# Weight splits further ahead in the MLP of a two-layer encoder trunk, paid for with one raw tile and one set of rotary tables

## The chip, the cores and the metric

The kernel runs on 1 core of a Trainium2 chip. The metric is the device time of one execution in microseconds (us). Before the change it is 2003.32 us, the median of 3 runs (2003.09 to 2005.98). The trace comes from one more execution, of 2003.99 us, whose profiled span is 2002.2 us.

## What is computed

256 tokens of width 2048 go through two layers in float32. Each layer normalises, makes one input projection whose columns belong to three attention groups (A: windowed, B: neighbourhood on a grid, C: global with normalised and rotated q and k), joins them through an output projection, and ends with a squared-ReLU MLP of hidden width 8192:

```python
for l in range(DEPTH):
    h = rmsnorm(x, norm_mix[l])
    proj = jnp.einsum('bsd,de->bse', h, w_in[l])
    ...
    x = x + jnp.einsum('bse,ed->bsd', mix, w_o[l])
    h = rmsnorm(x, norm_mlp[l])
    u = jax.nn.relu(jnp.einsum('bsd,df->bsf', h, w_up[l]))
    x = x + jnp.einsum('bsf,fd->bsd', u * u, w_down[l])
return rmsnorm(x, norm_final)
```

The rotary part of group C multiplies q and k with cosines and sines that are scaled by the gains `c_q_gain[l]` and `c_k_gain[l]`; the kernel keeps these products as tables.

## The kernel before

**Steps.** All four big products are a list of steps. A step loads 512 KB of weights into a raw tile (`load`, SP's DMA queue, tile `wraw`), splits it into a high and a low part (`split`: ScalarE casts `whi`, L1017; VectorE subtracts to get `wlo`, L1018), and multiplies both on TensorE (`mm`). The input projection's and output projection's steps are matmuls of L479, 12 of 128x512 each. The main loop at the end of the function issues, ahead of the matmuls of a step, the loads of up to six steps behind it (`LOOK_LOAD` = 7 counts the step itself) and the split of the next step (`LOOK_SPLIT` = 2). Where the running step has `fourth=False`, which are the steps of the MLP mix, the next two are split.

**Tiles.** There are five raw tiles, three `whi` and three `wlo`. Outside the MLP every fourth split goes into a further pair of tiles, `spare0` and `spare1`; in the MLP the same two tiles hold the weights B11 of the products.

**The MLP.** `up_steps` makes the hidden activations: a step has 8 matmuls of 512 columns (L679) and 8 of 256 (L684), and after every fourth step `evac` copies the result out (L657 on ScalarE, L658 on VectorE, then L659 to L666, L696 to L698 on both). `strassen_steps` makes half of the down projection by seven products P1 to P7 in place of eight (the Strassen-Winograd scheme), each in two halves h = 0, 1 (a and b below) of 6 matmuls (L801). Its weights are B11, sums of weight blocks (`sum_of`, L779, VectorE) and blocks that a DMA from GpSimd's queue adds onto a tile (`on_top`, L783). T1 is B11 + B12 and T2 is B22 + (B11 + B12) with blocks stored so that sums stand for differences; P2 reads its own block, P6 reads T2. A step's `look` says how many steps ahead its sum is made: 8 in general, 3 for the sum T1 (at P2), 5 − h for T2 (at P6). The steps are dealt out by a pattern: 22 steps, 14 of products and 8 of the up projection, make a half group, in the order P1a P2a U P1b P2b U P6a P6b U P7a U P7b P5a U P5b P4a U P4b P3a U P3b U. There are twelve half groups in a layer, then two groups with other patterns. When a product group is done, VectorE adds its bank onto x (`evac`, which calls `residual`, L221); the score banks `S` take turns.

**Order.** The order on each engine follows from the program's order and a scheduler that places instructions by their dependences. A few edges are written out: `sum_of` is issued after the last subtract, the table code after the last subtract at step 11. In each engine's queue the order is then fixed, and an instruction that waits holds up those behind it.

**Rotary tables.** `setup_tables` makes four pairs of tables once, `ctab` and `stab` for q and k of both layers (L133, L136), at about 41 us. `rope` reads them on GpSimd (L317 and L321).

Of the kernel before, what the change touches and what calls it, by code (L numbers as in the profile page):

```python
# [17 lines left out]
F32 = mybir.dt.float32  # L18
# [5 lines left out]
P = 128  # L24
D = 2048
L = 2
# [17 lines left out]
def tile_trunk(ctx: ExitStack, tc: tile.TileContext, x_in, xt_in, w_in, w_o, w_up, w_down,  # L44
# [29 lines left out]
    def spare(dt, h):  # L74

        return wp.tile([P, 2, 512], dt, tag=f"spare{h}", bufs=1, name=nm("spare"))
# [47 lines left out]
    def setup_tables():  # L124

        nc.vector.tensor_scalar(negsink, rp[:, :, 0:8], -1.0, None, op0=ALU.mult)
        for l in range(L):
            nc.vector.tensor_scalar(rp[:, l, 8:72], rp[:, l, 8:72], 0.125, None, op0=ALU.mult)
            for which, off in (("q", 8), ("k", 72)):
                g = rp[:, l:l + 1, off:off + 64]  # L130
                c = cp.tile([P, NT, 64], F32, name=f"ctab_{which}{l}")
                s = cp.tile([P, NT, 64], F32, name=f"stab_{which}{l}")
                nc.vector.tensor_mul(c, cos_t, g.to_broadcast([P, NT, 64]))  # L133
                for a in range(4):
                    b = a ^ 1
                    nc.vector.tensor_mul(s[:, :, 16 * a:16 * a + 16], sin_t[:, :, 16 * a:16 * a + 16],  # L136
                                         g[:, :, 16 * b:16 * b + 16].to_broadcast([P, NT, 16]))
                ctab[which, l], stab[which, l] = c, s
# [159 lines left out]
    def rope(raw, H, which, l, outs):  # L298
# [15 lines left out]
        ct, st = ctab[which, l], stab[which, l]  # L314
# [149 lines left out]
    class Step:  # L464


        def __init__(self, src, kk, n, pre, mm, fourth=True, loads=None, prep=None, raw=None,
                     look=0, ready=None):
            self.look, self.ready = look, ready
            self.src, self.kk, self.n, self.pre, self.mm, self.fourth = src, kk, n, pre, mm, fourth  # L470
            self.loads, self.prep, self.raw = loads or [], prep, raw
# [31 lines left out]
    def layer_steps(l):  # L503
# [143 lines left out]
        def up_steps(g):  # L647

            out_ = []
            for q in range(4 * g, 4 * g + 4):  # L650
# [18 lines left out]
                for s in range(4):  # L669
# [19 lines left out]
                    out_.append(Step(w_up[l, q * 4 + s], 4, 256, pre, mm, fourth=False))  # L689
# [10 lines left out]
        def down_steps(gs, j, ks=range(4)):  # L700
# [7 lines left out]
            for n, (g, k) in enumerate(tiles):  # L708
# [40 lines left out]
                out_.append(Step(w_down[l, ti], 2, 512, None, mm, fourth=gs == (7,)))  # L749
            return out_  # L750

        def strassen_steps(g, pair=0):
# [35 lines left out]
            for (name, lf, bk, fresh, dst), h in first + then:  # L788
                def mm(wh, wl, name=name, lf=lf, bk=bk, fresh=fresh, dst=dst, h=h):
# [14 lines left out]
                    if h == 1 and (name != "P2" or g == (5 if pair else 7)):  # L804
                        evac(o, *dst)
                        if g == 7 and name in ("P3", "P4"):
                            layer_end(l, dst[1])
                loads, prep, get, ready, look = [], None, None, None, 8
                if name == "P1":
                    loads = [(("B11", h), src(0, 0, h), lambda h=h: spare(F32, h))]  # L810
                    get = lambda h=h: raw["B11", h]
                elif name == "P2":
# [5 lines left out]
                    look = 3  # L818
# [6 lines left out]
                elif name == "P6":  # L825
# [6 lines left out]
                    look = 5 - h  # L832
# [14 lines left out]
                stp = Step(src(1, 0, h) if name == "P2" else None, 2, 512, None, mm, fourth=False, prep=prep,  # L847
# [143 lines left out]
    fourth = [0]  # L991

    def load(i, halves=False):
# [7 lines left out]
        w = wp.tile([P, s.kk, s.n], F32, tag="wraw", bufs=5, name=nm("wraw"))  # L1001
# [21 lines left out]
    warm = cp.tile([P, 512], F32R, name="warm")  # L1023
# [21 lines left out]
    for i in range(8):  # L1045
        load_xt()
        if i < 5:
            load(i, halves=i == 0)
    nl = 5
# [3 lines left out]
    for i, s in enumerate(steps):  # L1053
# [159 lines left out]
```

## Time and profile before

| quantity | value |
|---|---|
| median of 3 runs | 2003.32 us |
| profiled execution / its span | 2003.99 / 2002.2 us |
| TensorE matmul busy | 1976.5 us |
| VectorE busy | 1689.7 us |
| ScalarE busy | 1302.4 us |
| GpSimd busy | 381.2 us |
| mean DMA rate | 223 GB/s |

In the rows, PE is TensorE's matmul, PEld its weight load, DVE VectorE, ACT ScalarE, POOL GpSimd, and SPq a queue of DMA issues. A row of the timeline gives the start, the time taken, engine, line, operation, output<-inputs, and in brackets how long the engine was idle before it and on what it waited. A row of waits gives the total of a wait in us, how often it occurred and the longest. A row of windows gives the length of a stretch, the busy time of PE, PEld, DVE, ACT and POOL in it, the granted clock of TensorE (1.00 is full), the share of DMA time and GB/s. The page's DMA issues list the size and the median time from issue to landing.

### The profile page before, as it was taken

How to read it: one execution, taken by the hardware profiler on the slowest of the kernel's cores; microseconds unless marked ns; L12 is line 12 of the kernel's file. 1: busy time of each engine (PE TensorE's matmuls, PEld its weight loads, DVE VectorE, ACT ScalarE, POOL GpSimd, SP SyncE). 2: the span in 40 equal slices, each digit the busy share in tenths (PEclk: the TensorE clock that was granted, in tenths of full speed). 3: DMA queues.
4: the chain of work that ended last, by engine and by line, in shares of the span. 5: the costliest groups of instructions: out<-in, count | busy, mean ns of one | idle time of the engine just before them, and what ended most of it. 6: DMA issues, size and time to landing. Idle time of an engine off the chain costs nothing.

```text
span 2002.2 us, 28385 instructions
## 1 busy us (share of the span) xinstructions
PE 1976.5 (99%) x10054; PEld 1667.0 (83%) x10054; DVE 1689.7 (84%) x2119; ACT 1302.4 (65%) x1814; POOL 381.2 (19%) x444
## 2 busy tenths in 40 slices
PE   9999999999999999999999999999999999999998
PEld 7888888888888888888888888888888888888886
DVE  7777877899999999988857688778999999999887
ACT  7667756666666666666657677566666666666664
POOL 0674520000100001000008655100010000000000
PEclk9999999999999999999999999999999999999999
DMA  9755656788888878877756465557888888888774
GB/s 342 216 158 157 212 169 191 215 250 234 255 251 261 241 242 247 246 233 222 228 185 197 148 184 192 179 189 226 235 255 251 263 241 239 247 247 268 221 228 139
DMA packets 125753, 445.80 MB, mean 223 GB/s; under 512 B 14339, under 2 KB 16643, under 8 KB 125612
## 3 DMA queue, kind: packets, MB, share of 16 engines
q1 hardware_dynamic: 109052, 384.18, 56.7%
q0 software_dynamic: 16128, 58.73, 16.3%
q8 instruction: 79, 1.29, 0.3%
q10 hardware_dynamic: 432, 1.10, 0.1%
q14 instruction: 62, 0.51, 0.1%
HBM read 438.16 MB, written 2.11 MB: 220 GB/s over the span
## 4 chain that ended last, share of the span: by engine, by line
PE 92%; DVE 3%; ACT 3%; issue 1%; DMA 0%; SPq 0%; POOLq 0%; POOL 0%; DVEq 0%; ACTq 0%
PE mm L479 28%; PE mm L679 23%; PE S L801 21%; PE mm L684 12%; PE tr L801 4%; DVE wlo L1018 2%; ACT whi L1017 2%; PE tr L388 1%; PE tr L407 1%; PE S L351 1%; PE S L350 1%; PE tr L231 1%; ACT wide L657 0%; PE tr L263 0%; PE tr L400 0%
## 5 line engine op out<-in xcount | busy, mean ns | idle before, releaser
L1018 DVE TENSOR_TENSOR wlo<-wraw,whi 128x1024 fp32r<-128x1024 f32 (+1 forms) x481 | 592.0, 1233 | 146.0 <-ACT whi L1017 141.0
L1017 ACT CAST whi<-wraw 128x1024 fp32r<-128x1024 f32 (+1 forms) x481 | 502.9, 1048 | 240.1 <-PE mm L679 79.2
L679 PE MATMUL mm<-big,whi 128*128 128x512 f32 x2048 | 514.7, 391 | 0.0
L679 PEld LDWEIGHTS mm<-big,whi 128*128 128x128 f32 x2048 | 382.4, 188 | 79.8 <-ACT whi L1017 0.7
L479 PE MATMUL mm<-whi,big 128*128 128x512 f32 (+1 forms) x1404 | 423.4, 384 | 1.0 <-ACT whi L1017 1.0
L801 PE MATMUL S<-whi,big 128*128 128x512 f32 x1344 | 369.9, 397 | 9.7 <-ACT whi L1017 9.7
L479 PEld LDWEIGHTS mm<-whi,big 128*128 128x128 f32 x1404 | 260.2, 189 | 50.5 <-ACT whi L1017 2.3
L684 PEld LDWEIGHTS mm<-big,wlo 128*128 128x128 f32 x2048 | 279.7, 190 | 20.5
L684 PE MATMUL mm<-big,wlo 128*128 128x256 f32 x2048 | 286.2, 282 | 0.0
L801 PEld LDWEIGHTS S<-whi,big 128*128 128x128 f32 x1344 | 235.3, 189 | 59.8 <-ACT whi L1017 20.5
L479 PE MATMUL mm<-wlo,big 128*128 128x512 f32 (+1 forms) x702 | 253.8, 381 | 0.0
L783 POOL DMA_DIRECT2D side<-in_w_down_dram x56 | 48.9, 873 | 1001.9 <-ACT whi L1017 612.1
L801 PE MATMUL S<-wlo,big 128*128 128x512 f32 x672 | 210.9, 395 | 1.4
L1017 ACT CAST whi<-big 128x1024 fp32r<-128x1024 f32 x112 | 118.2, 1055 | 126.6 <-DVE big L779 58.4
L1018 DVE TENSOR_TENSOR wlo<-big,whi 128x1024 fp32r<-128x1024 f32 x112 | 136.7, 1221 | 44.0 <-ACT whi L1017 44.0
L1018 DVE TENSOR_TENSOR wlo<-side,whi 128x1024 fp32r<-128x1024 f32 x112 | 136.6, 1220 | 31.5 <-ACT whi L1017 31.2
L801 PEld LDWEIGHTS S<-wlo,big 128*128 128x128 f32 x672 | 124.9, 188 | 37.6 <-DVE wlo L1018 11.0
L1017 ACT CAST whi<-spare 128x1024 fp32r<-128x1024 f32 x112 | 117.7, 1051 | 53.0 <-PE S L801 41.7
L479 PEld LDWEIGHTS mm<-wlo,big 128*128 128x128 f32 x702 | 132.4, 189 | 23.4 <-DVE wlo L1018 0.3
L1017 ACT CAST whi<-side 128x1024 fp32r<-128x1024 f32 x112 | 117.5, 1049 | 46.5 <-PE S L801 42.9
L1018 DVE TENSOR_TENSOR wlo<-spare,whi 128x1024 fp32r<-128x1024 f32 x112 | 136.5, 1219 | 6.8 <-ACT whi L1017 6.6
L479 PE MATMUL mm<-spare,big 128*128 128x512 f32 (+1 forms) x606 | 140.3, 381 | 0.0
(153 smaller groups left out, 2224.2 us busy)
## 6 DMA issues: line engine op xcount, KB each, us to landing
wraw<-in_w_up_dram SPq DMA_DIRECT2D x256, 512.0 KB, 4.7
wraw<-in_w_in_dram SPq DMA_DIRECT2D x119, 512.0 KB, 3.8
side<-in_w_down_dram SPq DMA_DIRECT2D x112, 512.0 KB, 4.7
wraw<-in_w_down_dram SPq DMA_DIRECT2D x88, 512.0 KB, 5.3
wraw<-in_w_o_dram SPq DMA_DIRECT2D x64, 512.0 KB, 3.7
spare<-in_w_down_dram SPq DMA_DIRECT2D x56, 512.0 KB, 5.6
side<-in_w_down_dram POOLq DMA_DIRECT2D x56, 512.0 KB, 7.4
big<-in_w_down_dram POOLq DMA_DIRECT2D x56, 512.0 KB, 7.3
```

Source lines behind the costliest of these rows:

```text
L231: nc.tensor.transpose(psv[:, kk, t, :], x[:, t, c0:c0 + P], ident)
L350: nc.tensor.matmul(o, st, u.kh[:, kh, :], start=True, stop=False)
L351: nc.tensor.matmul(o, st, u.kl[:, kh, :], start=False, stop=True)
L388: nc.tensor.transpose(ps[:, c * P:(c + 1) * P], u.p[:, s, kb * P:(kb + 1) * P], ident)
L407: nc.tensor.matmul(ps, u.V[:, kb, u.kv, :, :], pt[:, kb, :], start=n == 0, stop=n == 3)
L479: nc.tensor.matmul(banks[t][:, 0:n], a, (wl if part == "hl" else wh)[:, i, :], start=first and i == 0 and part == "hh", stop=last and i == ...
L679: nc.tensor.matmul(box["b"][fs], wh[:, kk, fs * P:(fs + 1) * P], ht, start=s == 0 and kk == 0, stop=False, skip_group_check=True)
L684: nc.tensor.matmul(box["b"][fs][:, 0:256], wl[:, kk, fs * P:(fs + 1) * P], ht[:, 0:256], start=False, stop=s == 3 and kk == 3, skip_group_ ...
L783: nc.gpsimd.dma_start(tile, src(par, j, h).rearrange("p (k n) -> p k n", k=2), accum_op=ALU.add)
L801: nc.tensor.matmul(o, ops[i][a], w[:, i, :], skip_group_check=True, start=fresh and h == 0 and i == 0 and a == 0 and w is wh and (bk != "b ...
L1017: last_act[0] = nc.scalar.copy(h[:, part], w[:, part]).ins
L1018: last_lo[0] = nc.vector.tensor_sub(lo[:, part], w[:, part], f(h[:, part])).ins
```

## The change

Four `whi` and four `wlo` tiles take the place of three each; the trick with every fourth split goes, and `spare` becomes `first`, which holds B11 alone. `wraw` has four tiles, not five. A step marked `deep` (up projection, products, and the plain down steps that are not of the last group alone) has the next three steps split ahead of its matmuls; any other step has the next one. The sums for P2 and P6 get looks of 8 and 6. The rotary tables exist once for q and once for k; `layer_tables(1)` remakes them for the second layer at a place in the program late in layer 0's MLP. The tile `warm` moves to another pool, and the start loads four raw tiles ahead.

```diff
-    def spare(dt, h):
-        return wp.tile([P, 2, 512], dt, tag=f"spare{h}", bufs=1, name=nm("spare"))
+    def first_block(h):
+        return wp.tile([P, 2, 512], F32, tag=f"first{h}", bufs=1, name=nm("first"))
...
-        for l in range(L):
-            nc.vector.tensor_scalar(rp[:, l, 8:72], rp[:, l, 8:72], 0.125, None, op0=ALU.mult)
-            for which, off in (("q", 8), ("k", 72)):
...
-                ctab[which, l], stab[which, l] = c, s
+        nc.vector.tensor_scalar(rp[:, :, 8:72], rp[:, :, 8:72], 0.125, None, op0=ALU.mult)
+        for which in ("q", "k"):
+            ctab[which] = cp.tile([P, NT, 64], F32, name=f"ctab_{which}")
+            stab[which] = cp.tile([P, NT, 64], F32, name=f"stab_{which}")
+        layer_tables(0)
+
+    def layer_tables(l):
+        for which, off in (("q", 8), ("k", 72)):
+            g = rp[:, l:l + 1, off:off + 64]
+            c, s = ctab[which], stab[which]
+            nc.vector.tensor_mul(c, cos_t, g.to_broadcast([P, NT, 64]))
+            for a in range(4):
+                b = a ^ 1
+                nc.vector.tensor_mul(s[:, :, 16 * a:16 * a + 16], sin_t[:, :, 16 * a:16 * a + 16],
+                                     g[:, :, 16 * b:16 * b + 16].to_broadcast([P, NT, 16]))
...
                         evac(o, *dst)
+                        if (l, g, name) == (0, 7, "P1"):
+                            layer_tables(1)
...
-                    loads = [(("B11", h), src(0, 0, h), lambda h=h: spare(F32, h))]
+                    loads = [(("B11", h), src(0, 0, h), lambda h=h: first_block(h))]
...
-                    look = 3
                     ready = lambda h=h: ("P1", h) in done
...
-                    look = 5 - h
+                    look = 6
...
-        w = wp.tile([P, s.kk, s.n], F32, tag="wraw", bufs=5, name=nm("wraw"))
+        w = wp.tile([P, s.kk, s.n], F32, tag="wraw", bufs=4, name=nm("wraw"))
...
-        fourth[0] += s.fourth
-        if s.fourth and fourth[0] % 4 == 0:
-            h, lo = [spare(F32R, e).rearrange("p k n -> p (k n)").rearrange("p (k n) -> p k n", k=s.kk) for e in range(2)]
-        else:
-            h = wp.tile([P, s.kk, s.n], F32R, tag="whi", bufs=3, name=nm("whi"))
-            lo = wp.tile([P, s.kk, s.n], F32R, tag="wlo", bufs=3, name=nm("wlo"))
+        h = wp.tile([P, s.kk, s.n], F32R, tag="whi", bufs=4, name=nm("whi"))
+        lo = wp.tile([P, s.kk, s.n], F32R, tag="wlo", bufs=4, name=nm("wlo"))
...
-    warm = cp.tile([P, 512], F32R, name="warm")
+    warm = mid(F32R, 512)
...
-        if i < 5:
+        if i < 4:
             load(i, halves=i == 0)
-    nl = 5
+    nl = 4
...
-        while ns < min(len(steps), i + LOOK_SPLIT + (not s.fourth)):
+        while ns < min(len(steps), i + LOOK_SPLIT + 2 * s.deep):
```

Line numbers shift by four in the functions behind the tables: L779, L783, L801, L221 and L657 become L783, L787, L805, L225 and L661; the cast and the subtract stay at L1017 and L1018, the loads of L1004 become L1008 and those of the tiles L1001.

Three places of the order show what moves. The first is a half group of the MLP on VectorE, from the sums T1 (onto `spare` or `first`) and T2 (into `big`) to the subtracts of the halves of P6 (`wlo<-big`); `x<-S` is the evacuation. Before:

```order
L1018 TENSOR_TENSOR wlo_4591<-wraw_4528,whi_4590 128x1024 [waits DMAHW1_49,PE_49,Activation_49]
L779 TENSOR_TENSOR spare_4502<-spare_4502,side_4526 128x1024 [waits DMAHW5_49,DVE_49]
L779 TENSOR_TENSOR big_4595<-side_4564,spare_4439 128x1024 [waits DMAHW2_49]
L1018 TENSOR_TENSOR wlo_4615<-wraw_4541,whi_4614 128x1024 [waits DMAHW3_49,PE_49,Activation_49]
L221 SCALAR_TENSOR_TENSOR x<-S_3807,rsq,x 128x512 [waits PE_49]
L1018 TENSOR_TENSOR wlo_4628<-big_4595,whi_4627 128x1024 [waits Activation_49]
L779 TENSOR_TENSOR big_4631<-side_4576,spare_4502 128x1024 [waits DMAHW4_49]
L658 TENSOR_TENSOR wide_4661<-wide_4661,mm_4508 128x256 [waits Activation_49]
L1018 TENSOR_TENSOR wlo_4641<-big_4631,whi_4640 128x1024 [waits Activation_49]
```

and after:

```order
L1018 TENSOR_TENSOR wlo_4569<-wraw_4518,whi_4568 128x1024 [waits DMAHW2_49,PE_49,Activation_49]
L783 TENSOR_TENSOR first_4491<-first_4491,side_4516 128x1024 [waits DMAHW4_49,DVE_49]
L783 TENSOR_TENSOR big_4572<-side_4553,first_4428 128x1024 [waits DMAHW1_49]
L1018 TENSOR_TENSOR wlo_4583<-wraw_4531,whi_4582 128x1024 [waits DMAHW4_49,PE_49,Activation_49]
L783 TENSOR_TENSOR big_4586<-side_4566,first_4491 128x1024 [waits DMAHW3_49,DVE_49]
L1018 TENSOR_TENSOR wlo_4606<-big_4572,whi_4605 128x1024 [waits PE_49,Activation_49]
L225 SCALAR_TENSOR_TENSOR x<-S_3797,rsq,x 128x512 [waits PE_49]
L1018 TENSOR_TENSOR wlo_4619<-big_4586,whi_4618 128x1024 [waits Activation_49]
L1018 TENSOR_TENSOR wlo_4630<-wraw_4580,whi_4629 128x1024 [waits DMAHW5_49,PE_49,Activation_49]
L662 TENSOR_TENSOR wide_4650<-wide_4650,mm_4498 128x256 [waits Activation_49]
```

P6b's sum moved ahead of P6a's subtract, both subtracts of P6 and the next one moved ahead of the additions of the up-projection's copy (L658, now L662), and the evacuation moved behind P6a's subtract. ScalarE in the same place, with the casts of P6a, P6b and of the next up step, and the copies L657; before:

```order
L1017 CAST whi_4614<-wraw_4541 128x1024 [waits DMAHW3_49,DVE_49,PE_49]
L1017 CAST whi_4627<-big_4595 128x1024 [waits DVE_49,PE_49,Activation_49]
L657 COPY wide_4661<-mm_4508 128x256 [waits PE_49]
L657 COPY wide_4661<-mm_4509 128x256 [waits PE_49]
L1017 CAST whi_4640<-big_4631 128x1024 [waits DVE_49,Activation_49]
```

and after:

```order
L1017 CAST whi_4582<-wraw_4531 128x1024 [waits DVE_49,DMAHW4_49,PE_49,Activation_49]
L1017 CAST whi_4605<-big_4572 128x1024 [waits DVE_49,PE_49,Activation_49]
L1017 CAST whi_4618<-big_4586 128x1024 [waits DVE_49,PE_49,Activation_49]
L1017 CAST whi_4629<-wraw_4580 128x1024 [waits DMAHW5_49,PE_49,Activation_49]
L1017 CAST whi_4664<-side_4464 128x1024 [waits DMASW0_49,PE_49,Activation_49]
L661 COPY wide_4650<-mm_4498 128x256 [waits PE_49]
```

The two copies no longer stand between the two casts of P6, but behind four casts.

The second place is SP's queue at the start, which issues the tokens' tiles (`big<-in_xt_dram`), the weights and x. Before:

```order
L1034 DMA big_127<-in_xt_dram 128x512 [waits DMAHW2_49]
L1004 DMA wraw_129<-in_w_in_dram 128x1024 [waits DMAHW3_49]
L1034 DMA big_131<-in_xt_dram 128x512 [waits DMAHW4_49]
L1034 DMA big_133<-in_xt_dram 128x512 [waits DMAHW5_49]
L1034 DMA big_135<-in_xt_dram 128x512 [waits DMAHW6_49]
L1004 DMA wraw_157<-in_w_in_dram 128x1024 [waits DMAHW7_49,DVE_49]
```

and after:

```order
L1034 DMA big_127<-in_xt_dram 128x512 [waits DMAHW2_49]
L1034 DMA big_129<-in_xt_dram 128x512 [waits DMAHW3_49]
L1034 DMA big_131<-in_xt_dram 128x512 [waits DMAHW4_49]
L1034 DMA big_133<-in_xt_dram 128x512 [waits DMAHW5_49]
L1001 DMA first_3635<-in_w_down_dram 128x1024 [waits DMAHW6_49]
L1001 DMA first_3705<-in_w_down_dram 128x1024 [waits DMAHW7_49]
L1008 DMA wraw_155<-in_w_in_dram 128x1024 [waits DMAHW0_49,DVE_49]
L1008 DMA wraw_157<-in_w_in_dram 128x1024 [waits DMAHW1_49,DVE_49]
```

The fifth weight tile (`wraw_129`, now `wraw_155`) moved behind the last token tiles and behind the first two blocks B11 of the MLP (`first`), whose tiles nothing else uses.

The third place is VectorE in layer 0's mixing stage, where the remade tables stand, though the code calls for them in the MLP (L138 and L141 are the tables, with two pieces of what is around them):

```order
L1018 TENSOR_TENSOR wlo_876<-wraw_687,whi_875 128x1024 [waits DMAHW1_49,DVE_49,Activation_49]
L377 TENSOR_TENSOR sm_777<-sm_767,negsink 128x4 [waits DVE_49]
L138 TENSOR_TENSOR ctab_k<-cs,rp 128x128 [waits Pool_49]
L141 TENSOR_TENSOR stab_k<-cs,rp 128x2x16 [waits Pool_49] x4
L1018 TENSOR_TENSOR wlo_910<-wraw_705,whi_909 128x1024 [waits DMAHW2_49,Activation_49]
```

and further on, for q:

```order
L435 SCALAR_TENSOR_TENSOR big_1335<-mid_1171,gn,big_1335 128x256 [waits Activation_49] x2
L138 TENSOR_TENSOR ctab_q<-cs,rp 128x128 [waits Pool_49]
L141 TENSOR_TENSOR stab_q<-cs,rp 128x2x16 [waits Pool_49] x4
L361 TENSOR_REDUCE sm_1392<-S_1382 128x4 [waits PE_49]
L1018 TENSOR_TENSOR wlo_1452<-wraw_1289,whi_1451 128x1024 [waits DMAHW4_49,Activation_49]
```

Both table rows wait for GpSimd, and subtracts and softmax rows stand behind them; before the change VectorE has no tables here.

More of the change, by code (lines that the diff above doesn't have):

```diff
@@ L313, in rope @@
         t2 = big(F32, NT, H, 64)
-        ct, st = ctab[which, l], stab[which, l]
+        ct, st = ctab[which], stab[which]
         for t in range(NT):
@@ L464, in tile_trunk, with __init__ @@
     class Step:
-        def __init__(self, src, kk, n, pre, mm, fourth=True, loads=None, prep=None, raw=None,
+        def __init__(self, src, kk, n, pre, mm, deep=False, loads=None, prep=None, raw=None,
                      look=0, ready=None):
             self.look, self.ready = look, ready
-            self.src, self.kk, self.n, self.pre, self.mm, self.fourth = src, kk, n, pre, mm, fourth
+            self.src, self.kk, self.n, self.pre, self.mm, self.deep = src, kk, n, pre, mm, deep
             self.loads, self.prep, self.raw = loads or [], prep, raw
@@ L687, in mm @@
                             evac()
-                    out_.append(Step(w_up[l, q * 4 + s], 4, 256, pre, mm, fourth=False))
+                    out_.append(Step(w_up[l, q * 4 + s], 4, 256, pre, mm, deep=True))
             return out_
@@ L748, in down_steps @@
                 ti = (g * 4 + j) * 4 + k
-                out_.append(Step(w_down[l, ti], 2, 512, None, mm, fourth=gs == (7,)))
+                out_.append(Step(w_down[l, ti], 2, 512, None, mm, deep=gs != (7,)))
             return out_
```

11 lines of the change are left out of this document (1 added, 10 removed).

## The prediction

> **What bounds the kernel.** First the page's span, the busy times and the chain that ended last.
>
> ```profile
> span 2002.2 us, 28385 instructions
> PE 1976.5 (99%) x10054; PEld 1667.0 (83%) x10054; DVE 1689.7 (84%) x2119; ACT 1302.4 (65%) x1814; POOL 381.2 (19%) x444
> PE 92%; DVE 3%; ACT 3%; issue 1%; DMA 0%; SPq 0%; POOLq 0%; POOL 0%; DVEq 0%; ACTq 0%
> ```
>
> TensorE carries 92% of the chain. The change leaves its matmuls alone, so it can only win or lose time in which TensorE waits; VectorE's and ScalarE's 6% of the chain are such places. The view of waits names the waits of the Strassen products (L801):
>
> ```profile
> PEld S L801 <- ACT whi L1017: 20.5, 27, 2.5
> PEld S L801 <- DVE wlo L1018: 11.0, 22, 0.5
> PE S L801 <- ACT whi L1017: 9.7, 27, 2.3
> PEld S L801 <- DVE x L221: 2.1, 7, 0.5
> ```
>
> 27 times a product waits for the cast of its weights (L1017), 22 times for the subtract behind it (L1018). The timeline shows one of them, at product P6:
>
> ```profile
> 503.59 1.22 DVE L779 TENSOR_TENSOR big<-side,spare 128x1024 f32<-128x1024 f32 x1
> 504.44 1.09 PE L801 MATMUL S<-whi,big 128*128 128x512 f32 x4
> 504.52 0.65 ACT L657 COPY wide<-mm 128x256 f32<-128x256 f32 x2 [2.60 <-PE mm L684]
> 505.05 1.06 ACT L1017 CAST whi<-big 128x1024 fp32r<-128x1024 f32 x1
> 506.14 1.23 DVE L1018 TENSOR_TENSOR wlo<-big,whi 128x1024 fp32r<-128x1024 f32 x1 [0.47 <-ACT whi L1017]
> 506.16 1.20 PE L801 MATMUL S<-whi,big 128*128 128x512 f32 x4 [0.18 <-ACT whi L1017]
> 507.42 0.72 PE L801 MATMUL S<-wlo,big 128*128 128x512 f32 x2
> 507.98 2.02 PE L679 MATMUL mm<-big,whi 128*128 128x512 f32 x8
> 510.79 1.09 PE L801 MATMUL S<-whi,big 128*128 128x512 f32 x4
> 512.18 1.07 PE L679 MATMUL mm<-big,whi 128*128 128x512 f32 x4
> ```
>
> An undisturbed step of a product lasts 512.18 − 510.79 = 1.39 us. The two halves of P6 take 507.98 − 504.44 = 3.54, 0.76 more than 2.78. The reason is the row of work before: the sum of weights that P6b reads ends at 504.8 (503.59 + 1.22), ScalarE is then at the copies of an up-projection tile, casts from 505.05 to 506.1, and TensorE, due at 505.82, starts at 506.16; the low half, subtracted meanwhile, is late once more. The pattern of 22 steps returns every 42.27 us, twelve times in a layer. The first of a layer is longer, and one near the end of each layer much longer:
>
> ```profile
> 377.27 1.09 PE L801 MATMUL S<-whi,big 128*128 128x512 f32 x4
> 381.18 1.09 PE L679 MATMUL mm<-big,whi 128*128 128x512 f32 x4
> 889.28 1.23 DVE L666 TENSOR_TENSOR big<-wide,big 128x1024 fp32r<-128x1024 f32 x1 [1.17 <-ACT big L665]
> 890.43 1.22 DVE L779 TENSOR_TENSOR big<-side,spare 128x1024 f32<-128x1024 f32 x1
> 892.83 1.84 PE L801 MATMUL S<-whi,big 128*128 128x512 f32 x4 [2.27 <-ACT whi L1017]
> 1886.97 1.21 PE L801 MATMUL S<-whi,big 128*128 128x512 f32 x4 [2.25 <-ACT whi L1017]
> 463.00:505.27 42.27, 42.03 (x214) 35.23 (x213) 39.00 (x46) 27.86 (x33) 3.49 (x4) 1.00 0.84 250
> 870.00:897.00 27.00, 24.73 (x121) 20.87 (x120) 21.81 (x25) 13.96 (x16) 2.62 (x3) 0.94 0.70 198
> 1864.00:1891.00 27.00, 24.75 (x130) 21.05 (x129) 22.04 (x25) 13.82 (x16) 2.59 (x3) 1.00 0.70 196
> ```
>
> The first six rows are of the timeline, the last three of windows. At 378 us the excess is 381.18 − 377.27 − 2.78 = 1.13. At 890 the sum stands in VectorE's row behind L666, and TensorE idles 2.27 us; the window from 870 to 897 shows the granted clock at 0.94, which over 27 us is another 1.6. The same wait in layer 1 (2.25) left the clock at 1.00. In all: 20 × 0.76 = 15.2, 2 × 1.13 = 2.3, two at the end of the pattern that I take at half (0.7), 2.27 + 1.6 = 3.9, 2.3, and about 0.5 for the 27th: **24.9 us** of waiting for splits.
>
> **What the change removes.** With splits three steps ahead in place of two and P6's sums made six ahead, both sums and both casts of P6 stand ahead of the copies L657 in the queues. They then come some 2 us before they are used: P6b's cast no longer follows the two copies, and its sum has one subtract less ahead of it. The sum before 890 moves ahead of L666 in the same way. I count all 24.9; the lower bound is nothing (rival c). The cover is VectorE's spare time: 42.27 − 0.76 − 39.00 = 2.5 us in a half group (93% busy), and the change adds no work there. One raw tile fewer I cost at nothing:
>
> ```profile
> wraw<-in_w_up_dram SPq DMA_DIRECT2D x256, 512.0 KB, 4.7
> ```
>
> A half group draws ten raw tiles (eight of its steps are up-projection, two are P2) in 42 us. With four tiles a load can be issued once the tile four before it is split, on average 17 us ahead of its own split, and it lands in 4.7. Were that cover gone, each load would be late by up to one step of 2.8 us.
>
> **What it adds: the start.** Two 512 KB loads of the tiles `first` now stand on SP's queue ahead of the fifth weight tile.
>
> ```profile
> GB/s 0 0 17 162 357 361 294 239 229 311 403 393 376 403 410 417 423 413 410 406 423 386 382 396 430 375 420 416 396 410 416 416 430 410 410 416 423 423 437 430
> 17.73 1.05 ACT L1017 CAST whi<-wraw 128x1024 fp32r<-128x1024 f32 x1 [1.46 <-DMA wraw<-in_w_in_dram]
> 17.86 1.98 PE L479 MATMUL mm<-whi,big 128*128 128x512 f32 x8
> ```
>
> The cast at 17.73 waits for the sixth weight tile, so that one landed at 17.7. The transfers are full here (410 GB/s in the second half of the first 24 us: 1.28 us for 512 KB). In the new order the bytes up to the fifth tile are those that went before up to the sixth, plus one tile: it lands at 17.7 + 1.28 = 19.0, its cast ends at 20.0, and its step, due at 17.86, starts 2.2 us late. Nothing gives that back, since TensorE is the bound from there on: **+2.2**, and +0.3 for the evacuations behind it. Bounds 0 (the transfers are spread over the queue in a way I don't see) and 3.8 (one more transfer of 1.28).
>
> **What it adds: the tables.** The second layer's tables overwrite the first's, so VectorE's rows for them wait until GpSimd has read the old ones. They stand early in VectorE's queue, in layer 0's mixing stage: the k tables behind L377 at some 73 us, the q tables behind L435 at 129.
>
> ```profile
> 77.52 2.14 POOL L321 TENSOR_TENSOR big<-mid,stab_k 128x64 f32<-128x64 f32 x4
> 82.88 0.40 PE L479 MATMUL mm<-wlo,big 128*128 128x512 f32 x1
> 129.06 1.23 DVE L357 TENSOR_REDUCE sm<-S 128x4 f32<-128x1024 f32 x1
> 130.14 2.70 POOL L321 TENSOR_TENSOR big<-big,stab_q 128x128 f32<-128x128 f32 x4
> 132.12 0.56 ACT L368 ACTIVATE big<-S,sm,rq 128x256 f32<-128x256 f32 x1 [4.61 <-DVE sm L456]
> 133.76 0.56 ACT L368 ACTIVATE big<-S,sm,rq 128x256 f32<-128x256 f32 x1
> 135.84 0.28 PE L350 MATMUL S<-big,big 128*128 128x256 f32 x1
> 42.00 0.49 DVE L136 TENSOR_TENSOR stab_k<-cs,rp 128x32 f32<-128x32 f32 x4
> ```
>
> The k tables: GpSimd ends at 77.52 + 2.14 = 79.7. VectorE stands still for some 6.5 us, and the next subtract ends near 81, ahead of the matmul at 82.88 that reads it; the softmax rows behind it come 3 to 5 us later, and nothing on TensorE asks for them at once. Bounds 0 and 3; I take **0.3**, near the slack of the subtract. At 41 us, where layer 1's tables were made, VectorE saves some 0.8, under TensorE's work and so worth nothing. The q tables: GpSimd ends at 132.84, the tables take some 0.8 (the row at 42.00 has 0.49 for one of their parts). The reduce, at 129.06 before, starts near 133.0 at the earliest, 3.9 later, even counting the q tables as half over. The exponentials (132.12 to 134.3) move to about 136 to 138, and the scores (L350, 135.84), which overwrite what they read, from 135.84 to about 137.8: **+2.0**, bounds 0 and 4.
>
> **What is late next.** Each product group writes a bank that VectorE's L221 must have emptied. In the new order that evacuation stands behind one more subtract at P6 (1.23 us).
>
> ```profile
> 522.04 0.75 DVE L221 SCALAR_TENSOR_TENSOR x<-S,rsq,x 128x512 f32<-128x512 f32 x1
> 522.98 1.10 PE L801 MATMUL S<-whi,big 128*128 128x512 f32 x4
> ```
>
> Here 0.19 us lie between the evacuation's end (522.79) and the product that overwrites it. Following VectorE's new order by these durations I find 0.1 to 1.0 us left at each of the six groups, so up to 0.3 per half group; I take 0.05 × 24 = **1.2**.
>
> Sum: −24.9 + 2.5 + 0.3 + 2.0 + 1.2 = −18.9. From the profiled execution, 2003.99 us (1.8 around its span), that gives 1985.1; the median of the runs is 0.67 lower, so 1984.4: **1984**.
>
> A rule on the two new waits of 2 us. The row above shows the clock falling to 0.94 over 27 us behind an idle of 2.27, and not behind one of 2.25. The Trainium skill, "TensorE: Matmul & The Clock Gate", section "Why this matters for your kernels", puts the limit at idle gaps of about 3 us, below which matmuls keep the full clock. By that rule neither new wait would lower it; the row at 892.83 contradicts the figure, and by that row each could cost 1.6 more (3.2 in all, 1988). I leave it out of the sum and keep it in the range.
>
> **Rivals.**
> (a) The evacuation takes the split's place. Each half group keeps 0.2 to 0.5 us instead of 0.76, now as a wait for L221. For it: the 0.19 above and VectorE's 93%. Against: only 7 such waits in the trace. Price: 24 × 0.3 more = 7 us, about 1991.
> (b) The costs of the start and the tables are hidden or undone by slack I have not seen: −24.9 + 1.2, about 1980. For it: VectorE and ScalarE wait often in the first 140 us. Against: the wait for the tile is a matter of bytes.
> (c) The change doesn't do what it says: P6's sum needs its load and GpSimd's tiles, is still late, and all stays but the costs: 2003.3 + 4.8 = 2008. Against: VectorE reaches the sum in the new row ahead of P6a's subtract, 2 to 3 us before.
> (d) Slower: one evacuation of each half group falls behind a subtract of 1.23 us at the tightest place, where 0.19 is spare: 24 × 1.04 = 25 us, 2009. It decides from 24 × 0.79 us on, where it eats the gain of 18.9. VectorE's 2.5 spare us per half group speak against it, not its order.
>
> **Chances.** Forecast 0.58, (a) 0.20, (b) 0.10, (c) 0.05, (d) 0.07. About 0.2% (4 us) is what a measurement of this kernel can tell from no change. Faster by more than that: 0.87; within it: 0.04; slower: 0.09, being (c), (d) at their prices. The range runs from 1978, (b) with the 1.2 gone too, to 1993, (a) with both clock drops.
>
> **What would show it.** The waits of L801 for L1017 (27) and for L1018 (22) go to a few; the pattern's period falls from 42.27 to about 41.5 us; waits for L225, the evacuation's new line, show (a) or (d) by their count. The fifth step of the first projection starts near 20.0 instead of 17.86. VectorE shows an idle of 4 to 7 us ahead of L138 and L141, released by GpSimd, and TensorE one of 2 us near 136. If the period stays at 42.2, the removal was wrong; if the waits near 20 and 136 are absent, the additions.

## The result, and the profile after

The changed kernel takes 1993.71 us (median of 4 runs, 1989.49 to 1995.61) against 2003.45 before: a ratio of 0.9946 with the interval 0.9928 to 0.9964. In a second set of 5 runs it took 1990.32 (1989.69 to 1991.64) against 2004.26: 0.9933, 0.9920 to 0.9945. The forecast was 1984, so the gain came, at half of its forecast size in the first set and seven tenths in the second. The first median lies 0.7 us above the upper end of the forecast's range (1993), the second inside it. The profiled execution of the first set was its slowest, 1995.61 us.

The page of after, first line and the chain that ended last:

```profile
span 1993.8 us, 28309 instructions
...
PE 96%; DMA 2%; DVE 1%; ACT 1%; issue 1%; SPq 0%; POOL 0%; POOLq 0%; DVEq 0%; ACTq 0%
```

VectorE and ScalarE have lost two thirds of their 6%, and DMA, at 0% before, has 2%. The view of waits of after, TensorE's rows (total us, times, longest):

```profile
PEld S L805 <- DVE x L225: 15.1, 48, 0.4
...
PE tr L267 <- ACT big L526: 4.3, 2, 3.2
...
PE mm L483 <- ACT whi L1017: 2.3, 2, 2.1
...
PE S L355 <- DMA mid<-mid: 1.8, 1, 1.8
```

The 27 waits of the products for casts and the 22 for subtracts are gone, all of them. In their place stand 48 short waits for the evacuation (L225; 7 of them before), and longer ones outside the MLP. The timeline of after shows where:

```profile
18.87 1.04 ACT L1017 CAST whi<-wraw 128x1024 fp32r<-128x1024 f32 x1 [4.73 <-DMA wraw<-in_w_in_dram]
62.51 0.36 PE L355 MATMUL S<-mid,big 128*128 128x256 f32 x1 [1.83 <-DMA mid<-mid]
142.89 0.39 PE L354 MATMUL S<-big,big 128*128 128x256 f32 x1 [1.05 <-ACT big L372]
164.62 0.63 PE L392 MATMUL tr<-ident,big 128*128 128x128 f32 x4 [0.80 <-DVE big L274]
510.92 1.09 PE L805 MATMUL S<-whi,big 128*128 128x512 f32 x4
526.71 1.22 DVE L1018 TENSOR_TENSOR wlo<-big,whi 128x1024 fp32r<-128x1024 f32 x1
527.84 0.75 DVE L225 SCALAR_TENSOR_TENSOR x<-S,rsq,x 128x512 f32<-128x512 f32 x1
528.65 0.76 PEld L805 LDWEIGHTS S<-whi,big 128*128 128x128 f32 x4 [0.29 <-DVE x L225]
552.71 1.09 PE L805 MATMUL S<-whi,big 128*128 128x512 f32 x4
1205.48 0.47 PE L267 MATMUL tr<-ident,big 128*128 128x128 f32 x1 [3.19 <-ACT big L526]
```

The rows at 510.92 and 552.71 are the first halves of P6 of two half groups, 41.79 us apart; before the change they were 42.26 apart (504.44 and 546.70). So a half group gained 0.47 us, of the 0.76 that its wait had cost.

Where the rest went is best read by counting. TensorE runs 10054 matmuls in every one of these kernels, so the start of the n-th in one trace less that in the trace of before says how far a kernel is ahead or behind at that point. The table has these differences in us, worked out from the traces: by the 400th matmul (82 us in before), what is added between the 650th and the 1000th (133 to 201 us, where the q tables are), what the MLPs of both layers add (352 to 931 and 1325 to 1920 us), and the whole difference of the spans.

| kernel | by 82 us | 133 to 201 us | both MLPs | span | median of the runs |
|---|---|---|---|---|---|
| after, first profile | +5.8 | +2.4 | −19.9 | −8.4 | 1993.71 |
| after, second profile | +4.3 | +2.4 | −20.2 | −13.9 | 1990.32 |
| looks_only | 0.0 | 0.0 | −21.0 | −21.1 | 1983.15 |
| raw4 | +3.1 | +0.1 | −1.1 | +2.7 | 2006.82 |
| first_late | +3.2 | +2.4 | −20.0 | −14.8 | 1989.86 |
| tables_late | +4.2 | 0.0 | −20.0 | −16.2 | 1988.50 |
| both_late | +3.1 | 0.0 | −19.8 | −16.5 | 1987.46 |
| deep2 | +4.7 | +2.4 | −25.5 | −17.8 | 1987.90 |
| two_banks | +0.5 | 0.0 | −28.7 | −28.8 | 1974.96 |
| after_two_banks | +4.6 | +2.4 | −29.3 | −22.8 | 1981.56 |
| raw5_lo3 | +6.2 | −0.2 | +2.0 | +11.0 | 2014.41 |

The first profile of after has 3.6 us more between 1150 and 1266 us, at the row of 1205.48: 2.0 us of longer wait and 1.7 us of clock, which is at half from 1205.34 to 1208.75. No other kernel of the table has it there. In raw5_lo3 another 2.8 us lie behind the last matmul.

### The profile page after: what moved, and what is told of

The parts are those of the page before. It is cut to its first block, busy times and chain, and to the rows that moved or that the text cites. A ratio compares the mean times of both kernels' runs of the same rounds, so it can differ in the third digit from the quotient of the medians.

```text
span 1993.8 us, 28309 instructions
## 1 busy us (share of the span) xinstructions
PE 1972.2 (99%) x10054; PEld 1669.3 (84%) x10054; DVE 1687.8 (85%) x2118; ACT 1304.9 (65%) x1814; POOL 381.0 (19%) x444
## 3 DMA queue, kind: packets, MB, share of 16 engines
q8 instruction: 79, 1.29, 0.3%
## 4 chain that ended last, share of the span: by engine, by line
PE 96%; DMA 2%; DVE 1%; ACT 1%; issue 1%; SPq 0%; POOL 0%; POOLq 0%; DVEq 0%; ACTq 0%
PE mm L483 27%; PE S L805 24%; PE mm L683 23%; PE mm L688 12%; PE tr L805 4%; PE tr L392 1%; PE tr L411 1%; PE S L355 1%; DMA wraw<-in_w_in_dram 1%; PE S L354 1%; PE tr L235 1%; DMA wraw<-in_w_o_dram 0%; PE tr L267 0%; ACT big L372 0%; PE tr L404 0%
## 5 line engine op out<-in xcount | busy, mean ns | idle before, releaser
L1018 DVE TENSOR_TENSOR wlo<-wraw,whi 128x1024 fp32r<-128x1024 f32 (+1 forms) x529 | 654.0, 1240 | 219.1 <-ACT whi L1017 211.9
L1017 ACT CAST whi<-wraw 128x1024 fp32r<-128x1024 f32 (+1 forms) x529 | 550.8, 1048 | 347.1 <-PE S L805 142.3
L483 PE MATMUL mm<-whi,big 128*128 128x512 f32 (+1 forms) x1808 | 545.4, 385 | 2.3 <-ACT whi L1017 2.3
L483 PEld LDWEIGHTS mm<-whi,big 128*128 128x128 f32 x1808 | 335.9, 189 | 66.4 <-ACT whi L1017 3.7
L805 PE MATMUL S<-whi,big 128*128 128x512 f32 x1344 | 369.8, 397 | 0.0
L483 PE MATMUL mm<-wlo,big 128*128 128x512 f32 (+1 forms) x904 | 329.8, 382 | 0.0
L805 PEld LDWEIGHTS S<-whi,big 128*128 128x128 f32 x1344 | 235.8, 189 | 51.9 <-DVE x L225 15.1
L787 POOL DMA_DIRECT2D side<-in_w_down_dram x56 | 48.9, 873 | 1003.9 <-DVE first L783 791.9
L805 PE MATMUL S<-wlo,big 128*128 128x512 f32 x672 | 207.9, 390 | 0.0
L1017 ACT CAST whi<-big 128x1024 fp32r<-128x1024 f32 x112 | 117.7, 1051 | 128.4 <-DVE big L783 100.0
L483 PEld LDWEIGHTS mm<-wlo,big 128*128 128x128 f32 x904 | 171.4, 190 | 30.3
L805 PEld LDWEIGHTS S<-wlo,big 128*128 128x128 f32 x672 | 126.2, 188 | 28.4
L1018 DVE TENSOR_TENSOR wlo<-first,whi 128x1024 fp32r<-128x1024 f32 x112 | 136.6, 1220 | 8.1 <-ACT whi L1017 4.9
L1018 DVE TENSOR_TENSOR wlo<-big,whi 128x1024 fp32r<-128x1024 f32 x112 | 136.2, 1216 | 4.7 <-ACT whi L1017 4.7
L1018 DVE TENSOR_TENSOR wlo<-side,whi 128x1024 fp32r<-128x1024 f32 x112 | 136.4, 1218 | 4.1 <-ACT whi L1017 3.3
L1017 ACT CAST whi<-first 128x1024 fp32r<-128x1024 f32 x112 | 117.4, 1048 | 34.1 <-PE mm L683 23.6
L1017 ACT CAST whi<-side 128x1024 fp32r<-128x1024 f32 x112 | 117.4, 1048 | 28.2 <-PE S L805 21.8
L225 DVE SCALAR_TENSOR_TENSOR x<-S,rsq,x 128x512 f32<-128x512 f32 x168 | 125.1, 745 | 0.4
```

The costliest lines, as they stand in the source:

```text
L225: nc.vector.scalar_tensor_tensor(xs, bank, rsq[:, l, int(sign < 0), t:t + 1], xs, op0=ALU.mult, op1=ALU.add)
L483: nc.tensor.matmul(banks[t][:, 0:n], a, (wl if part == "hl" else wh)[:, i, :], start=first and i == 0 and part == "hh", stop=last and i == ...
L787: nc.gpsimd.dma_start(tile, src(par, j, h).rearrange("p (k n) -> p k n", k=2), accum_op=ALU.add)
L805: nc.tensor.matmul(o, ops[i][a], w[:, i, :], skip_group_check=True, start=fresh and h == 0 and i == 0 and a == 0 and w is wh and (bk != "b ...
L1017: last_act[0] = nc.scalar.copy(h[:, part], w[:, part]).ins
L1018: last_lo[0] = nc.vector.tensor_sub(lo[:, part], w[:, part], f(h[:, part])).ins
```

## The experiments

**The sums alone.** looks_only is the kernel before with nothing of the change but its two looks.

```diff
-                    look = 3
...
-                    look = 5 - h
+                    look = 6
```

> The kernel before with nothing but the two looks of the change (T1 8 steps ahead, T2 6 steps ahead); three whi and wlo tiles, five raw tiles, splits two ahead, tables and start as before. Theory L (the looks removed the wait at P6b): the waits of L801 for L1017 and L1018 go, the half group falls from 42.27 to 41.5-41.7 us, no new waits at 18, 60, 141 and 1205 us, so about 2003.4 - 24 = 1979 us (1977 to 1985). Theory D (the third step of split depth removed it): the half group stays at 42.0 or more and the time at 1998 or more.

It took 1983.15 us: 0.9895 of before, 0.9880 to 0.9910, and faster than the change itself. In its view of waits no product waits for a split, and the evacuation's row is the one that after has:

```profile
PEld S L801 <- DVE x L221: 13.5, 45, 0.4
```

The P6 rows of its timeline, one half group apart:

```profile
502.51 1.09 PE L801 MATMUL S<-whi,big 128*128 128x512 f32 x4
...
544.25 1.09 PE L801 MATMUL S<-whi,big 128*128 128x512 f32 x4
```

41.74 us, with five raw tiles, three `whi` and `wlo`, and splits two ahead. The MLPs gain 21.0, as much as by the whole change. Theory L holds; with T1 and T2 made earlier both casts of P6 stand ahead of the copies, and no deeper split is needed for that.

**The raw tile alone.** raw4 is the kernel before with four raw tiles.

```diff
-        w = wp.tile([P, s.kk, s.n], F32, tag="wraw", bufs=5, name=nm("wraw"))
+        w = wp.tile([P, s.kk, s.n], F32, tag="wraw", bufs=4, name=nm("wraw"))
...
-        if i < 5:
+        if i < 4:
...
-    nl = 5
+    nl = 4
```

> The kernel before with four raw tiles in place of five (and four loads ahead at the start), nothing else. Theory R (the raw tile is not free): the cast before the output projection's step near 1199 us waits for its load, the wait of L263 at 1205 us grows from 1.15 by 2 us or more, and the softmax start near 57 us may wait for its DMA as it does in the changed kernel (2.1 us): 2005.5 to 2010 us. The forecast's reading (the tile is free): no new wait over 0.5 us, 2003.4 plus or minus 1.5 us.

2006.82 us, 1.0015 of before (1.0006 to 1.0025): slower, by 3.1 us at 82 us, and not where I expected it. The wait at 1205 us stayed as it was; what came was one at 33.75 us. From the timeline of raw4:

```profile
28.21 1.15 ACT L203 ACTIVATE big<-x,zero 128x1024 f32<-128x1024 f32 x1 [2.25 <-DMA x<-in_x_dram]
33.75 0.33 PE L263 MATMUL tr<-ident,big 128*128 128x128 f32 x1 [1.04 <-ACT big L572]
```

and the windows from 20 to 40 us (length; busy PE, PEld, DVE, ACT, POOL; clock; DMA share; GB/s), of before:

```profile
20.00:40.00 20.00, 20.00 (x126) 17.31 (x125) 13.84 (x22) 16.64 (x25) 0.71 (x1) 1.00 0.93 351
```

and of raw4:

```profile
20.00:40.00 20.00, 18.71 (x102) 15.94 (x101) 11.95 (x16) 16.03 (x25) 0.71 (x1) 0.91 0.79 282
```

The start is the stretch in which the transfers are the limit: 0.93 of the engines' time before. With one raw tile fewer a weight load has to wait for a tile, and what follows in SP's queue is issued later: here the second load of the tokens x, at 19.17 us in place of 15.11, on which the statistics L203 and the transposes wait. The transfers' share falls to 0.79. TensorE idles 1 us, and the clock of 0.91 over these 20 us makes another 1.8 of it.

**B11 later.** first_late issues the loads of `first` behind the weight load ahead of them in the program.

```diff
-            nc.sync.dma_start(w, src.rearrange("p (k n) -> p k n", k=2))
+            with tc.issue_after(last_load[0]):
+                nc.sync.dma_start(w, src.rearrange("p (k n) -> p k n", k=2))
```

> The changed kernel with the loads of B11 issued after the weight load ahead of them in the program, so not in the first 20 us. Theory S (1 MB ahead of the fifth weight tile makes TensorE wait): the wait of 2.06 us at 19.96 us and the low clock behind it go (cluster of 3.9 us), the fifth step starts before 18.5 us; if the wait of 2.1 us near 62 us is the same backlog it goes too: 1993.7 - 3.9 to 1993.7 - 6.4, 1987 to 1990 us. Rival (four raw tiles hold back the fifth tile): the fifth step still starts after 19 us, and the time stays within 1.5 us of 1993.7.

1989.86 us, 0.9938 of before (0.9920 to 0.9955). The wait at 19.96 us is gone, and the shift by 31 us is 0.0. But the wait near 60 us for the DMA `mid<-mid` stayed (1.8 us), so by 82 us the kernel has still lost 3.2. That is as much as raw4 loses, but in another place and by waits alone: the clock stays at 1.00 here, while of raw4's 3.1 us more than half is clock. So the equal size is partly chance. Half of theory S holds, the fifth step; the backlog at 60 us isn't B11's.

**The tables later.** tables_late makes layer 1's tables behind the last subtract that the program has issued.

```diff
-                            layer_tables(1)
+                            with tc.issue_after(last_lo[0]):
+                                layer_tables(1)
```

> The changed kernel with the second layer's tables remade after the last subtract issued so far, so in layer 0's MLP, not in the mixing stage. Theory T (VectorE's wait for GpSimd ahead of the tables costs TensorE): the waits of TensorE at 141.5 (1.2 us) and 163 us (1.0 us) go, 1993.7 - 2.3 = 1991.4 us; in the MLP two tables take some 0.8 us of VectorE once. Rival (these waits come from the later start or the fewer raw tiles): they stay within 0.3 us, and the time within 1 us of 1993.7.

1988.50 us, 0.9921 (0.9906 to 0.9936). The waits at 141 and 163 us are gone, and with them 2.4 us: theory T, at the size that it named.

**Both.** both_late has the last two edits together.

> The changed kernel with the loads of B11 issued behind the weight load ahead of them and the tables remade behind the last subtract: the two added waits taken out together, four raw tiles and splits three ahead left. Theory A (the costs add up): 1993.7 - 2.6 (first_late's shift by 82 us against the changed kernel's, 3.2 against 5.8) - 2.4 (141 and 163 us) = 1988.7 or less, down to 1986.5 where the wait near 60 us is small as well; what it keeps against looks_only (1983.2) is the raw tile's 3.1 us and nothing of the split depth. Rival (split depth gains something in the MLP): below 1984.

1987.46 us, 0.9918 (0.9904 to 0.9931). By 82 us +3.1, nothing at the tables, −19.8 in the MLPs: the costs add up, and what is left of them is the raw tile's 3.1. Of the split depth no gain shows, the MLPs being 1.2 behind looks_only. Beside tables_late the median falls by 1.0 us, near the 1.1 that the table shows by 82 us, though the two intervals overlap.

**The changed kernel again.**

> The changed kernel once more, for a second profile and more times. Reading N (the 3.6 us that the first profile shows at 1197 to 1210 us, a cast waiting for its w_o load and TensorE 3.2 us behind it, come and go between executions): the second profile has 1.2 to 1.6 us there as the kernels first_late and tables_late do, and a span near 1990. Reading W (they belong to the order of this kernel): they are there again.

The wait at 1205 us is 1.1 in this profile, as in before, and the span 1988.3: reading N. One profile of the changed kernel in two has it, and the second set of runs is 3.4 us below the first. The wait of 2.1 us at 20 us is in both profiles, but the clock behind it is not. Windows from 16 to 28 us, of after in the first profile:

```profile
16.00:28.00 12.00, 9.94 (x37) 7.72 (x36) 7.01 (x10) 9.13 (x15) 0.00 (x0) 0.86 1.03 413
```

and in the second:

```profile
16.00:28.00 12.00, 9.92 (x44) 7.91 (x43) 7.00 (x10) 9.27 (x15) 0.00 (x0) 1.00 1.02 412
```

0.14 of 12 us is 1.7 us, nearly the difference at 31 us between the two (+3.8 and +2.1).

**One step less depth.** deep2 is the changed kernel with the next two steps split ahead in the MLP, not three.

```diff
-        while ns < min(len(steps), i + LOOK_SPLIT + 2 * s.deep):
+        while ns < min(len(steps), i + LOOK_SPLIT + s.deep):
```

> The changed kernel with splits two steps ahead in the MLP as before the change, all else of it kept. Theory L (the looks did it, the depth nothing): the MLP's share stays, within 1.5 us of the changed kernel's 1993.7 or of after_again, whichever profile is compared. Theory D (depth matters beside the looks): the waits of L805 for L1017 come back and 3 us or more are lost.

1987.90 us, 0.9922 (0.9907 to 0.9937). Neither theory had this: the MLPs gain 25.5 us, 5.3 more than with the third step. The wait for the evacuation, in deep2:

```profile
PEld S L805 <- DVE x L225: 6.6, 24, 0.3
```

24 in place of 48. There are two places in a half group. The one that stays in deep2 is P4a, in the rows of after at 526.71 to 528.65: it waits for the evacuation of P5, which ends at 528.59. The one that goes is the first product of the next seven. After has there

```profile
540.09 1.22 DVE L1018 TENSOR_TENSOR wlo<-wraw,whi 128x1024 fp32r<-128x1024 f32 x1
541.23 0.74 DVE L225 SCALAR_TENSOR_TENSOR x<-S,rsq,x 128x512 f32<-128x512 f32 x1
542.02 0.76 PEld L805 LDWEIGHTS S<-whi,big 128*128 128x128 f32 x4 [0.39 <-DVE x L225]
```

and deep2

```profile
538.41 0.74 DVE L225 SCALAR_TENSOR_TENSOR x<-S,rsq,x 128x512 f32<-128x512 f32 x1
539.07 2.35 DVE L1018 TENSOR_TENSOR wlo<-wraw,whi 128x1024 fp32r<-128x1024 f32 x2
539.64 0.78 PEld L805 LDWEIGHTS S<-whi,big 128*128 128x128 f32 x4
```

With the third step of depth a subtract for a later step stands ahead of the evacuation; with two steps it stands behind. looks_only, two ahead as well but with three `whi` and `wlo` tiles, has 45 such waits; there a sum (L779) stands ahead of the evacuation. No run tells what the fourth `whi` and `wlo` alone do to that order. In deep2 the P6 rows are 41.54 us apart:

```profile
509.24 1.09 PE L805 MATMUL S<-whi,big 128*128 128x512 f32 x4
...
550.78 1.09 PE L805 MATMUL S<-whi,big 128*128 128x512 f32 x4
```

**Two banks in two tiles.** The two product banks are halves of one tile, so a product on one waits until VectorE has read the other. two_banks is looks_only with a tile for each:

```diff
-                        keep["S"] = score_banks().rearrange("p (b i) n -> p b (i n)", i=2)
-                    box["a"], box["d"] = keep["S"][:, flip], keep["S"][:, 1 - flip]
+                        keep["S"] = [score_banks().rearrange("p (b i) n -> p b (i n)", i=2)[:, 0], tr_bank()]
+                    box["a"], box["d"] = keep["S"][flip], keep["S"][1 - flip]
```

> looks_only with the two product banks in two tiles (one half of the score tile, and a bank of the other pool) in place of the two halves of one tile, so that a product no longer waits for the evacuation of the other bank; everything else as in looks_only. Theory E (what is left in the MLP are waits for L221, held for the whole tile): the 45 waits of L801 for L221 (13.5 us of weight-load idle) fall under 10, the half group falls by 0.2 us or more, 1983.2 - 24 x 0.2 = 1978 us (1976 to 1980). Rival (the remaining excess is the matmuls' own spacing, or the up projection's third bank pair is missed): 1983 or more.

1974.96 us, 0.9854 of before (0.9841 to 0.9868): below the expected range, and the fastest of all. The longest of TensorE's rows among its waits are these; none of them, and none of the shorter ones, is of a product:

```profile
PEld tr L263 <- ACT big L522: 3.5, 4, 1.6
PE tr L263 <- ACT big L522: 2.3, 2, 1.1
PE tr L1028 <- DVE warm L1023: 1.6, 1, 1.6
```

The half group falls to 41.38 us (`S` and `tr` are the two tiles, which take turns):

```profile
501.88 1.09 PE L801 MATMUL tr<-whi,big 128*128 128x512 f32 x4
...
543.26 1.09 PE L801 MATMUL S<-whi,big 128*128 128x512 f32 x4
```

The same edit on the changed kernel, after_two_banks:

> The changed kernel with the two product banks in two tiles, as two_banks has them; splits three ahead, four raw tiles, loads and tables as in the change. Theory E (what the changed kernel leaves in the MLP, and what the third step of depth costs against deep2, are waits for the evacuation L225): the 48 waits of L805 for L225 go, the MLP's shift against before goes from -20.3 (after_again) to -27 or more, 1990.3 - 7 to 1990.3 - 9, so 1981 to 1983 us. Rival (the depth costs something else, VectorE's or the loads' time): the MLP stays above -25.5, what deep2 has with 24 such waits, 1985 us or more.

1981.56 us, 0.9891 (0.9876 to 0.9906). No product waits for the evacuation, and the MLPs gain 29.3 us, 9.1 more than the change. So the evacuation was what the third step had cost, and with that gone the changed kernel's MLPs are 0.6 us ahead of two_banks: the depth, with its tiles, is worth no more than that.

**Five raw tiles in the changed kernel.** raw5_lo3 takes the room from the fourth `wlo`.

```diff
-        w = wp.tile([P, s.kk, s.n], F32, tag="wraw", bufs=4, name=nm("wraw"))
+        w = wp.tile([P, s.kk, s.n], F32, tag="wraw", bufs=5, name=nm("wraw"))
...
-        lo = wp.tile([P, s.kk, s.n], F32R, tag="wlo", bufs=4, name=nm("wlo"))
+        lo = wp.tile([P, s.kk, s.n], F32R, tag="wlo", bufs=3, name=nm("wlo"))
```

The start loads five raw tiles ahead again.

> The changed kernel with five raw tiles, as before, the room taken from the fourth wlo; all else kept (B11 early, tables early, splits three ahead as far as three wlo let them). Theory R (the start up to 82 us loses 3.1 us to the fourth raw tile's absence, as in raw4, and 1.2 to the early B11): the shift of TensorE at 82 us against before falls from 4.3 (after_again) to 0.5 to 2.0, and the DMA rate from 20 to 40 us rises from 320 to 340 GB/s or more. Rival (the early B11 loads alone make the wait near 60 us): 3.5 or more stay. The waits at 141 and 163 us stay at 2.4 in both; the MLP may lose time to the third wlo.

2014.41 us, 1.0054 (1.0037 to 1.0071). The expectation failed on both sides of the kernel. The DMA rate from 20 to 40 us is 355 GB/s, as theory R said, but the shift at 82 us is 6.2. From its timeline:

```profile
30.35 1.15 ACT L207 ACTIVATE big<-x,zero 128x1024 f32<-128x1024 f32 x1 [1.80 <-DMA x<-in_x_dram]
...
36.77 2.33 PE L267 MATMUL tr<-ident,big 128*128 128x128 f32 x8 [2.81 <-ACT big L576]
```

With the queue full and 1 MB of B11 ahead, x is what comes late: its statistics start at 30.35 (26.88 in before), and the transposes wait 2.8 us. The clock is at half from 35.26 to 42.09 us, another 3.4. So this run doesn't price the raw tile. In the MLP the gain is gone as well:

```profile
PEld S L805 <- ACT whi L1017: 17.8, 24, 0.9
PE S L805 <- DVE x L225: 12.9, 22, 0.7
```

There are 22 waits of the matmuls for the evacuation, up to 0.7 us each, and the weight loads wait for casts again, 24 times. That splits three ahead, with subtracts that wait for one of three `wlo` tiles, push the evacuation back fits this, and would be rival (d) of the prediction in a kernel that has its condition; which of the two waits sets the pace here was not tested.

## Why the prediction was right, and where it was not

**What bounds the kernel, and what goes:** right. All 27 waits for casts went, the long ones at 890 and 1886 us among them. The cause named was half right: the sums' places in the queues did it, the split depth had no part (looks_only).

**The evacuation, +1.2:** the mis-sized term, and the largest. I followed VectorE's new order by durations and gave it 0.05 us for a half group. The forecast had a half group at 42.26 − 0.76 + 0.05 = 41.55; it is 41.79, so the term is 0.29, or 7.0 us for 24 half groups, and rival (a), priced at 7 us more than the forecast, is what came. Two steps went wrong. One is a reading: the 0.19 us between the evacuation's end and the product at 522.98 was taken for slack. The weight loads of before show that there was none:

```profile
521.62 1.09 PEld L679 LDWEIGHTS mm<-big,whi 128*128 128x128 f32 x5
522.85 0.79 PEld L801 LDWEIGHTS S<-whi,big 128*128 128x128 f32 x4
```

The first of these ends at 522.71, and the next begins 0.14 us later, when the evacuation (522.79) is done; elsewhere some 0.04 us lie between two weight loads. So this product already waited, in every half group, below what the view of waits lists. Nor does it overwrite what that evacuation reads: it writes the other bank of the same tile. The other is that I put the price on the extra subtract at P6 alone; the waits of after are elsewhere in the half group (528.65 and 542.02 above). deep2 shows that the third step of depth makes half of them, and after_two_banks that all hang on the two banks being one tile.

**The start, +2.5:** the fifth tile's cast was put at 19.0 to 20.0 us and stands at 18.87 to 19.9; TensorE idles 2.06 us. The clock behind it was kept for the range, and came in one of two profiles. That range has a slip: (a) with both clock drops is 1991 + 3.2, so 1994 and not 1993.

**One raw tile fewer, at nothing:** wrong. The step failed where it was worked out for the MLP alone, with 17 us between loads; the tile is missed in the first 60 us, where the transfers are the limit. raw4 measures 3.1 us for it. Of the 4.3 to 5.8 us that the changed kernel has lost by 82 us, some 3.1 are the raw tile's and the rest B11's with the clock behind its wait, as far as first_late and both_late (3.2 and 3.1 without early B11) tell them apart. The terms don't simply add: where in the first 60 us a wait shows changes from kernel to kernel, and tables_late and after_two_banks, with the same wait and the same low clock as the first profile of after, have lost 4.0 and 4.1 us by 31 us but only 4.2 and 4.6 by 82, since their wait near 60 us is 0.5 and 0.7 in place of 1.8.

**The tables, +2.3:** 2.4, and tables_late shows them to be the cause. The mechanism for q was as told (scores waiting for the exponentials, 1.05 us at 142.89), with a second wait of 0.8 at 164.6 that I had not seen. The first place cost 1.3 us, not 2.0, the second 1.1, and the k tables nothing in place of 0.3; that the sum agrees so well is luck.

**The sum.** Put together: −24.9 + 2.5 + 2.3 + 1.2 was forecast. Measured in the second profile: −20.2 in the MLPs, +4.3 by 82 us, +2.4 at the tables, −0.4 elsewhere, in all −13.9. In the MLPs the forecast's −24.9 and +1.2 are −23.7: the twenty half groups in the middle of the two MLPs gained 9.8 us of the 14.2 forecast for them, and the ends of the pattern 10.4 where 9.5 was forecast. The first profile adds 1.5 by 82 us, where its clock was low, and the 3.6 at 1205 us. Of that wait the runs show only that it comes and goes; the cast that began it waited 1.64 us for a load of w_o, with four raw tiles, and why that load was late is open.

## What to carry to other kernels

A deeper split moves work ahead in a queue that others share; before paying for buffers, try moving only the one instruction that is late, here two sums. A tile that is spare in the steady state may be the one that keeps the transfers busy in the start, so its price is to be worked out for each stage. And where two banks are halves of one tile, look whether a write to one waits for the reader of the other: two tiles took away 7.7 to 9.1 us here, at the price of one bank more, since half of the old tile stays empty.

## What the runs showed of the hardware

The same idle of TensorE, 2.04 to 2.08 us near 20 us with nothing else changed there, was followed by a granted clock of 0.86 over 16 to 28 us in three profiles (after, tables_late, after_two_banks) and of 1.00 in two (after_again, deep2). The cost, 1.7 us, is nearly that of the idle itself. The windows of after show the low clock in full:

```profile
17.50:20.91 3.41, 1.35 (x6) 0.81 (x5) 0.97 (x1) 2.04 (x4) 0.00 (x0) 1.00 1.02 408
20.91:24.32 3.41, 3.41 (x10) 2.61 (x9) 3.41 (x7) 3.41 (x7) 0.00 (x0) 0.50 1.03 422
24.32:27.73 3.41, 3.41 (x16) 2.82 (x16) 2.63 (x4) 3.41 (x6) 0.00 (x0) 1.00 1.02 412
```

It is half for 3.41 us. It is half again from 1205.34 us, which is 347 times 3.413 us later, and in the other traces, too, the changes of the clock lie whole steps of 3.41 us apart. The Trainium skill's "TensorE: Matmul & The Clock Gate", section "What's actually happening", has the gate look at windows of some 3.4 us that run freely and lower the clock after an idle one, so that it matters where in a window an idle falls. The traces agree with the length, and with windows whose place differs from run to run. They do not agree with a wholly idle window: the one from 17.50 to 20.91 has 1.35 us of matmuls in it.

So the same idle can be followed by either clock. In after, tables_late and after_two_banks a single window holds 2.06, 2.04 and 2.01 us of it. In after_again a boundary cuts it (counted back in these steps from 1982.09 us, where the clock falls at the end of the kernel):

```profile
16.01:19.42 3.41, 1.74 (x8) 1.12 (x6) 0.00 (x0) 0.69 (x1) 0.00 (x0) 1.00 1.02 407
19.42:22.83 3.41, 3.00 (x13) 2.51 (x14) 3.02 (x4) 3.41 (x7) 0.00 (x0) 1.00 1.03 419
```

The first window has 1.67 us without matmuls, the second 0.41, and the clock stays. In deep2 they have 1.88 and 0.18. The two waits of before that the prediction set side by side differ in the same way: 2.26 us of idle in the window from 889.72 to 893.13, with half the clock behind it, and 1.69 in the one from 1883.00 to 1886.41, without. Idle time alone is not the whole rule: in raw4 a window with 1.29 us of it, from 31.79 to 35.20, where the transposes run, was followed by half the clock too, and no run here shows why.
